# Both parts of the moving tokens in one 512-column pass, added up when the bank is read

## The chip, the cores and the metric

The kernel runs on one core of a Trainium2 chip. The metric is the device time of one launch in microseconds (us). TensorE (PE in the profile) does the matrix products out of on-chip memory into PSUM banks of 128 partitions by 512 float32 columns; VectorE (DVE), ScalarE (ACT) and GpSimd (POOL) work beside it, and DMA queues bring the weights from DRAM.

## What is computed

A trunk of four layers over 256 tokens of width 1024. Each layer has a mixer, a feed-forward part and a gated embedding, each with norms around it; the mixers are differential attention (layers 0 and 3), a sparse attention with compressed, selected and windowed keys (layer 1, "nsa") and an attention with forget gates (layer 2, "fox"). The change touches products of two kinds only, of all tokens with a weight matrix:

```python
# differential attention: q and k of 1024 columns each, v
q, k, v = jnp.split(h @ w_in, 3, axis=-1)
# nsa: queries, six key and value projections, gates
proj = h @ w_in
q = proj[..., :nq]
# blocks of 32 tokens are compressed by a small network
return jax.nn.gelu(blk @ w1) @ w2
# feed-forward: width 4096, squared relu
return jnp.square(jax.nn.relu(h @ w1)) @ w2
```

## The kernel before, in words

**Split products.** All values are float32. A factor is split into a high part (rounded to the engine's float32r form) and a low part (the rest), and `three` makes a product of a chunk of 128 rows out of three matmuls: high by high, low by high, high by low. Weights are split on the chip: a DMA brings a piece of 512 KB into a `raw` buffer, ACT copies the high part into `wh` (L148), DVE subtracts it for the low part `wl` (L149). Each engine takes its instructions in the order in which the program lists them.

**Tokens as the moving operand.** The transposed tokens lie in two tiles `hT` (high and low; tag `big`, 1024 features in KD = 8 chunks by 256 tokens). `lin_b` computes 256 columns of the result, transposed: two blocks of 128 columns, for each of them 8 chunks, for each chunk `three` with 128x128 weights standing and 256 token columns moving. The two blocks fill the two halves of one bank of tag `pj`. One ACT instruction reads the whole bank: L975 in the feed-forward part, L436 (`evac`) for q and k, L892 in nsa. `q_pair` of nsa does the same with its own weights. There are 78 such banks in a launch: 48 in the feed-forward part, 24 for q and k of the two differential layers and fox, 6 in nsa.

**Weights as the moving operand.** The out projection (`lin_a`), the second feed-forward matrix (`down`) and the gate have tokens standing and weight columns moving, 512 at a time. `up_tok` does the first feed-forward matrix in this way for the first two of eight groups of 512 columns, in two passes of 256 columns.

**Banks.** PSUM has 8 banks: 4 for `acc`, 2 for `pj`, 2 for `wk` (transposes and small products). In nsa `pj` also holds the sums of the compression (`compress_up`, L698) and of the attention's outputs.

**Order.** The order of an engine's instructions is fixed when the program is built. Strings such as `SEQ` give the order of projections and attention steps of a mixer; `LAG` says by how many products a transpose is put off so that its operands are ready. In the feed-forward part a group runs two `lin_b`, then 48 matmuls of `down` for the group before.

Of the kernel before, what the change touches and what calls it, by code (L numbers as in the profile page):

```python
# [12 lines left out]
F32R = mybir.dt.float32r  # L13
# [29 lines left out]
LAG = {0: {'o': ((0, 0), (27, 27)), 'd': ((6, 6), (10, 10)), 'g': ((0, 0), (0, 1)), 'u': ((15,), (10,)), 'i': ((0,), (2,))}, 1: {'o': ((10, 10), (24, 24)), 'd': ((9, 9), (10, 10)), 'g': ((0, 0), (0, 0)), 'u': ((13,), (12,)), 'i': ((13,), (1,))}, 2: {'o': ((10, 11), (24, 24)), 'd': ((10, 10), (7, 7)), 'g': ((0, 0), (9, 9)), 'u': ((15,), (13,)), 'i': ((0,), (1,))}, 3: {'o': ((0, 0), (27, 27)), 'd': ((6, 6), (14, 14)), 'g': ((0, 0), (0, 0)), 'u': ((15,), (10,)), 'i': ((0,), (0,))}}  # L43
# [43 lines left out]
class Trunk:  # L87
# [29 lines left out]
    def big(self, dt=F32R):  # L117
        return self.t([P, KD, S], "big", 4, dt)
# [38 lines left out]
    def unit(self, src, k0, nk, c0, nc):  # L157
        """Rows of chunks k0..k0+nk and columns c0..c0+nc, split: [128, nk, nc]."""
        v = src[k0 * P : (k0 + nk) * P, c0 : c0 + nc].rearrange("(c p) n -> p c n", p=P)
        return self.split(self.raw(v, [nk, nc]), [nk, nc])  # L160

    def panel(self, src, c0, nc, nk, early=()):
        """All of 1024 rows in units of nk chunks; [k] gives chunk k's parts [128, nc]."""
        us = list(early)
        us += [self.unit(src, k, min(nk, KD - k), c0, nc) for k in range(len(us) * nk, KD, nk)]
        return [tuple(z[:, k % nk, :] for z in us[k // nk]) for k in range(KD)]

    def three(self, out, l, r, first, last):
# [3 lines left out]
        mm(out, l[0], r[1], start=False, stop=last)  # L172
        for e in self.queue:
            e[0] -= 1
# [4 lines left out]
    def later(self, n, key, fn):  # L179
        """Runs fn, which fills a part of key's tiles, after n more products, to issue behind them."""  # L180
# [6 lines left out]
    def flush(self, keys):  # L187
        """Before keys' tiles are read: runs what still has to fill them."""
        while any(e[1] in keys for e in self.queue):
            self.queue.pop(0)[2]()  # L190

    def tok(self, aT, k, t):
        if self.queue:
            self.flush([(id(aT[0]), t)])
        return tuple(z[:, k, t * P : (t + 1) * P] for z in aT)
# [26 lines left out]
    def transpose_split(self, src, hi, lo, t, scale=None, n=KD, c0=0, lag=()):  # L222
        """src [128 tok, n*128] -> hi/lo[:, c0 + c, t*128:(t+1)*128]."""
# [23 lines left out]
    def rms_halves(self, halves):  # L247
        """1 / rms of [half 0, half 1]; each half's square is taken when it is ready."""
# [14 lines left out]
    def prenorm(self, t, g, hT, lag=()):  # L263
        """After the last change of x[t]; takes its halves one after the other."""
# [30 lines left out]
    def startnorm_(self, t, g, hT):  # L295
        """prenorm of the input as it arrives; the second step transposes."""
# [24 lines left out]
    def lin_a(self, src, c0, aT, done, mix, pj=False, cuts=None, early=()):  # L321
        """y[t] = a @ src[:, c0 : c0 + 1024]; token tile 0 runs before tile 1."""
# [12 lines left out]
    def mul_a(self, y, a, w, first, mix):  # L335
        """y += a @ w over a list of chunks. The last ones end the sum, its first half mix chunks ahead of its second."""
# [19 lines left out]

# [12 lines left out]
    def bias_rows(self):  # L369
        """The bias of every distance, one row per head, then once per query row at a pitch of SKEW."""  # L370
# [24 lines left out]
    def bias_blocks(self):  # L395
        """The bias of the compressed blocks: [query, head, block], kept in DRAM."""
# [12 lines left out]
    def bias_load(self, h0):  # L409
        """-bias and mask of heads h0..h0+3: [query, head, j], j the distance 128 + i - j."""  # L410
# [43 lines left out]
    def diff(self, i, ia, hT):  # L454
# [25 lines left out]
        oT = (self.big(), self.big())  # L480
# [51 lines left out]
    def scores(self, q, k, qs, w):  # L532
        """Negated scores of 4 heads; heads on different rows of the array go to different banks."""
# [7 lines left out]
    def pipeline(self, items):  # L541
        """Software pipeline over generators: each step starts one and moves every open one by a stage."""
# [7 lines left out]
    def heads(self, w_in, w_out, hT, item, seq):  # L550
        """Runs the steps of seq: q/k + pair projects, p does half of the embedding's product, b the block bias,
        Q/K + pair loads the weights of its projection, O a chunk of the output projection's, two digits start
        the item of a pair and a token tile."""
# [3 lines left out]
        def items():  # L557
            for z in seq.replace(".", " ").split():
                if z[0] in "qkQK":
# [7 lines left out]
                    self.evac(qk[u][:, w], self.lin_b(w_in, w * D + 256 * u, hT, ws[w, u]), 1.0 if w else -0.125)  # L567
# [13 lines left out]
    def fox(self, i, hT):  # L581
# [41 lines left out]
        oT = (self.big(), self.big())  # L623
# [43 lines left out]
    def split_out(self, o, oT, c0, n, t):  # L667
        oh, ol = [z[:, c0 : c0 + n, t * P : (t + 1) * P] for z in oT]
# [3 lines left out]
    def compress_blocks(self, kind, kT):  # L672
        """Blocks of 32 tokens, two tokens' 64 features on the partitions: [(token, d), pair, group, block of 16]."""
# [19 lines left out]
    def compress_up(self, kind, blk, ph):  # L693
        """First layer of the compression: [(group, block), hidden] on a half of the partitions."""
# [8 lines left out]
    def compress_gelu(self, ph):  # L703
        """gelu of both kinds' hidden layers, transposed: [hidden, half, kind, group, block of 32]."""
# [40 lines left out]
    def nsa(self, i, hT):  # L745
# [79 lines left out]
        oT = (self.big(), self.big())  # L825
# [12 lines left out]
        def q_pair(ap):  # L838
# [3 lines left out]
            for r2 in range(2):  # L842
                o = self.pj()
                for rr in range(2):
                    r = 2 * r2 + rr
                    for k in range(KD):
                        st = [z[:, r, 2 * (k % 2) : 2 * (k % 2) + 2, :].rearrange("p g d -> p (g d)") for z in us[k // 2]]
                        self.three(o[:, rr * S : (rr + 1) * S], st, self.both(hT, k), k == 0, k == KD - 1)
                nc.scalar.activation(q[:, 2 * r2 : 2 * r2 + 2, :].rearrange("p a b -> p (a b)"), o, AF.Copy, scale=-0.125)
# [40 lines left out]
        for z, c in ((0, 512), (1, 1024)):  # L890
            o = self.lin_b(w_in, C0 + c, hT)
            nc.scalar.activation(ksw[:, :, z, :], o.rearrange("p (a b) -> p a b", a=2), AF.Copy)  # L892
# [71 lines left out]
    def mlp(self, i, hT, done):  # L964
# [191 lines left out]
```

## Time and profile before

| | before |
|---|---|
| time, median of 3 runs | 1440.13 us (1440.06 to 1442.18) |
| profiled execution: span | 1449.6 us, 9.5 us over the median of the runs |
| TensorE matmuls | 1411.0 us, 97%, 8814 instructions |
| TensorE weight loads | 1225.6 us, 85% |
| VectorE | 855.8 us, 59%, 1495 instructions |
| ScalarE | 755.1 us, 52%, 1239 instructions |
| GpSimd | 71.9 us, 5% |

How to read it: the span is that of one execution under the profiler; no other time of that execution is recorded, so differences worked out from its rows are taken off or put onto the median of the runs. TensorE is busy nearly all of the time. A matmul's record runs from its start to the end of its passage through the array, and the next one starts before that, so records overlap; how long one holds the engine is read from the distance between starts.

### The profile page before, as it was taken

The page shows a single profiled execution, that of the slowest core. Times are in us where ns is not written, and L with a number is a line of the kernel's source. Part 1 is how long each engine was busy: PE and PEld are TensorE (multiplying, and loading weights), DVE is VectorE, ACT ScalarE, POOL GpSimd, SP SyncE. Part 2 cuts the span into 40 slices and gives each one's busy share as a digit, 9 for nine tenths or more (in the row PEclk, how much of TensorE's full clock was granted, in tenths as well). Part 3 has the DMA queues.
Part 4 walks back from the last instruction along what each step waited for, and adds up shares of the span by engine and source line. Part 5 has one row for each costly group of instructions (what it writes and reads, how often), then busy time and mean ns, then how long its engine had stood idle before and what let it go on. Part 6 is the DMA issues. An engine that isn't in the chain of part 4 may idle for free.

```text
span 1449.6 us, 22594 instructions
## 1 busy us (share of the span) xinstructions
PE 1411.0 (97%) x8814; PEld 1225.6 (85%) x8814; DVE 855.8 (59%) x1495; ACT 755.1 (52%) x1239; POOL 71.9 (5%) x116
## 2 busy tenths in 40 slices
PE   8589999999999999999999999999999999999998
PEld 6588898998888678998987987998988987999987
DVE  5265765556637656655566555755557577855545
ACT  4255555444625565554446555645446656644443
POOL 1000200000100001000001000000001001100000
PEclk9888999999999899999999999999999999999999
DMA  8564465655575204655645742765646643655642
GB/s 298 177 209 136 136 217 173 202 190 180 164 216 177 77 30 146 225 185 173 202 160 157 257 138 87 233 191 173 203 138 213 221 141 109 213 194 175 203 146 73
DMA packets 155042, 251.41 MB, mean 173 GB/s; under 512 B 10294, under 2 KB 119782, under 8 KB 154936
## 3 DMA queue, kind: packets, MB, share of 16 engines
q1 hardware_dynamic: 144312, 236.44, 50.1%
q10 hardware_dynamic: 10624, 13.53, 3.0%
q8 instruction: 69, 1.13, 0.3%
q14 instruction: 37, 0.30, 0.1%
HBM read 247.61 MB, written 4.43 MB: 174 GB/s over the span
## 4 chain that ended last, share of the span: by engine, by line
PE 68%; issue 21%; DMA 3%; POOL 3%; DVE 2%; ACTq 2%; ACT 2%; DVEq 0%; SPq 0%; POOLq 0%
PE pj L170 11%; PE pj L171 10%; PE pj L172 10%; PE acc L170 9%; PE acc L171 9%; PE acc L172 9%; PE wk L234 2%; PE acc L538 2%; DMA nb<-skew 2%; ACTq L383 2%; PE acc L907 1%; POOL small L213 1%; PE pj L698 1%; PE wk L513 1%; PE wk L658 1%
## 5 line engine op out<-in xcount | busy, mean ns | idle before, releaser
L149 DVE TENSOR_TENSOR wl<-raw,wh 128x1024 fp32r<-128x1024 f32 x421 | 509.9, 1221 | 356.4 <-ACT wh L148 342.6
L148 ACT ACTIVATE wh<-raw 128x1024 fp32r<-128x1024 f32 x421 | 441.9, 1057 | 364.4 <-PE acc L171 149.8
L170 PE MATMUL pj<-big,wh 128*128 128x256 f32 x1248 | 357.2, 286 | 11.8 <-ACT wh L148 11.8
L171 PE MATMUL pj<-big,wl 128*128 128x256 f32 x1248 | 356.2, 285 | 1.1 <-DVE wl L149 1.1
L172 PE MATMUL pj<-big,wh 128*128 128x256 f32 x1248 | 355.5, 285 | 0.0
L170 PEld LDWEIGHTS pj<-big,wh 128*128 128x128 f32 x1248 | 241.1, 193 | 16.2 <-ACT wh L148 12.3
L171 PEld LDWEIGHTS pj<-big,wl 128*128 128x128 f32 x1248 | 241.1, 193 | 5.0 <-DVE wl L149 2.2
L172 PEld LDWEIGHTS pj<-big,wh 128*128 128x128 f32 x1248 | 241.1, 193 | 0.3
L170 PE MATMUL acc<-wh,s 128*128 128x512 f32 x512 | 200.3, 391 | 0.0
L171 PE MATMUL acc<-wh,s 128*128 128x512 f32 x512 | 199.6, 390 | 0.0
L172 PE MATMUL acc<-wl,s 128*128 128x512 f32 x512 | 199.3, 389 | 0.0
L170 PE MATMUL acc<-wh,big 128*128 128x512 f32 (+2 forms) x344 | 132.0, 384 | 0.0
L171 PE MATMUL acc<-wh,big 128*128 128x512 f32 (+2 forms) x344 | 131.1, 381 | 0.0
L172 PE MATMUL acc<-wl,big 128*128 128x512 f32 (+2 forms) x344 | 130.3, 380 | 0.0
L172 PEld LDWEIGHTS acc<-wl,s 128*128 128x128 f32 x512 | 96.1, 188 | 20.3
L170 PEld LDWEIGHTS acc<-wh,s 128*128 128x128 f32 x512 | 96.2, 188 | 18.9
L171 PEld LDWEIGHTS acc<-wh,s 128*128 128x128 f32 x512 | 96.3, 188 | 18.8
L170 PE MATMUL pj<-wh,big 128*128 128x256 f32 (+1 forms) x320 | 100.3, 315 | 0.3 <-ACT big L241 0.2
L171 PE MATMUL pj<-wh,big 128*128 128x256 f32 (+1 forms) x320 | 98.7, 309 | 0.3 <-DVE big L242 0.3
L172 PE MATMUL pj<-wl,big 128*128 128x256 f32 (+1 forms) x320 | 98.3, 307 | 0.0
L432 ACT ACTIVATE s<-s,small 128x128 f32<-128x128 f32 (+1 forms) x160 | 70.7, 446 | 33.8 <-DVE small L428 29.2
L170 PEld LDWEIGHTS acc<-wh,big 128*128 128x128 f32 x344 | 65.6, 191 | 12.6 <-issue 1.0
(209 smaller groups left out, 1545.6 us busy)
## 6 DMA issues: line engine op xcount, KB each, us to landing
raw<-in_mlp_w_dram SPq DMA_DIRECT2D x256, 512.0 KB, 3.9
raw<-in_da_w_in_dram SPq DMA_DIRECT2D x48, 512.0 KB, 5.5
raw<-in_ple_gate_w_dram SPq DMA_DIRECT2D x32, 512.0 KB, 3.5
raw<-in_fox_w_in_dram SPq DMA_DIRECT2D x24, 512.0 KB, 4.1
raw<-in_nsa_w_in_dram SPq DMA_DIRECT2D x18, 512.0 KB, 4.7
g<-in_norm_g_dram SPq DMA_DIRECT2D x16, 512.0 KB, 5.3
raw<-in_da_w_out_dram SPq DMA_DIRECT2D x16, 512.0 KB, 3.3
nb<-skew ACTq DMA_DIRECT2D x12, 512.0 KB, 4.8
```

The lines of the kernel that those rows point to most:

```text
L148: self.nc.scalar.activation(wh, w, AF.Copy),
L149: self.nc.vector.tensor_tensor(wl, w, wh.bitcast(F32), op=ALU.subtract),
L170: mm(out, l[0], r[0], start=first, stop=False)
L171: mm(out, l[1], r[0], start=False, stop=False)
L172: mm(out, l[0], r[1], start=False, stop=last)
L213: nc.gpsimd.tensor_scalar(me, ms, EPS, 1.0, op0=ALU.add, op1=ALU.mult)
L234: z = nc.tensor.transpose(pt[:, c * P : (c + 1) * P], src[:, (b + c) * P : (b + c + 1) * P], self.ident)
L383: self.dq[QS[1]].dma_start(sk, src)
L432: nc.scalar.activation(e[:, b, :], e[:, b, :], AF.Exp, bias=m[:, b : b + 1], scale=-1.0, accum_out=s[:, b : b + 1])
L513: nc.tensor.matmul(po[:, hh * P : (hh + 1) * P], at[:, hh, kb, :], vs[kb][:, h * P : (h + 1) * P], start=kb == 0, stop=kb == nk - 1,)
L538: self.nc.tensor.matmul(sc[c][:, hh * w : (hh + 1) * w], q[cs, hh, qs], k[cs, hh, :w], start=True, stop=True)
L658: nc.tensor.matmul(po[c * HD : (c + 1) * HD, hh * P : (hh + 1) * P], vs[kb][:, h * HD : (h + 1) * HD], at[:, hh, kb, :], start=kb == 0, st ...
```

## The change

`pair` takes the place of `three` where tokens move. The high and the low part of the tokens become one tile of two planes, and the high weights meet both in one matmul of 2 x 256 columns, whose result fills the two halves of a bank; the low weights meet the high part in a second matmul of 256 columns, added to the first half. Each block of 128 result columns now has a `pj` bank of its own. ACT copies the second half out, then DVE adds the first half; in the feed-forward part the relu moves into the DVE instruction that squares. `up_tok` takes 512 weight columns in a pass. The numbers in `LAG` that count products of this kind are halved.

```diff
-    def big(self, dt=F32R):
-        return self.t([P, KD, S], "big", 4, dt)
+    def big(self):
+        z = self.t([P, 2, KD, S], "big", 2, F32R)
+        return z[:, 0], z[:, 1], z
...
+    def pair(self, out, l, aT, k, first, last):
+        mm = self.nc.tensor.matmul
+        a = self.both(aT, k)[0]
+        mm(out.rearrange("p (z n) -> p z n", z=2), l[0], aT[2][:, :, k, :], start=first, stop=False)
+        mm(out[:, :S], l[1], a, start=False, stop=last)
+        self.tick()
...
     def lin_b(self, src, c0, hT, w=None):
         if w is None:
             w = self.panel(src, c0, 256, 4)
-        o = self.pj()
         for b in range(2):
             bs = slice(b * P, (b + 1) * P)
+            o = self.pj()
             for k in range(KD):
-                self.three(
-                    o[:, b * S : (b + 1) * S], (w[k][0][:, bs], w[k][1][:, bs]), self.both(hT, k), k == 0, k == KD - 1,
-                )
-        return o
+                self.pair(o, (w[k][0][:, bs], w[k][1][:, bs]), hT, k, k == 0, k == KD - 1)
+            yield o
...
     def evac(self, dst, o, scale=1.0):
-        self.nc.scalar.activation(dst.rearrange("p a b -> p (a b)"), o, AF.Copy, scale=scale)
+        self.nc.scalar.activation(dst, o[:, S:], AF.Copy, scale=scale)
+        self.nc.vector.scalar_tensor_tensor(dst, o[:, :S], scale, dst, op0=ALU.mult, op1=ALU.add)
...
             for b in range(2):
-                o = self.lin_b(w1, 512 * gi + 256 * b, hT)
                 z = self.m2([P, 512])
-                nc.scalar.activation(z, o, AF.Relu)
+                for c, o in enumerate(self.lin_b(w1, 512 * gi + 256 * b, hT)):
+                    zc = z[:, c * S : (c + 1) * S]
+                    nc.scalar.activation(zc, o[:, S:], AF.Copy)
+                    nc.vector.tensor_tensor(zc, zc, o[:, :S], op=ALU.add)
                 q = self.m2([P, 512])
-                nc.vector.tensor_tensor(q, z, z, op=ALU.mult)
+                nc.vector.scalar_tensor_tensor(q, z, 0.0, z, op0=ALU.max, op1=ALU.mult)
...
-                w[gi] = [self.panel(w1, 512 * gi + 256 * b, 256, 4) for b in range(2)]
+                w[gi] = self.panel(w1, 512 * gi, 512, 2)
...
-                    for b in range(2):
-                        for k in range(KD):
-                            self.three(o[:, b * 256 : (b + 1) * 256], self.tok(hT, k, t), w[gi][b][k], k == 0, k == KD - 1)
+                    for k in range(KD):
+                        self.three(o, self.tok(hT, k, t), w[gi][k], k == 0, k == KD - 1)
```

In the changed program the weights' split is at L150 and L151 (148 and 149 before), `evac` at L448 (ACT) and L449 (DVE), the first step of the softmax at L439 (428 before), L704 is L690 of before, L646 and L647 are L632 and L633.

VectorE at the start of layer 0's attention, before: the low parts of the weights (`wl`), then the first step of the softmax, which reads the scores `acc` and the bias `nb`.

```order
L149 TENSOR_TENSOR wl_92_477<-raw_90_474,wh_91_476 128x1024
L149 TENSOR_TENSOR wl_95_483<-raw_93_480,wh_94_482 128x1024
L149 TENSOR_TENSOR wl_109_611<-raw_107_608,wh_108_610 128x1024
L428 ISA s4_99_494,small_100_495<-acc_97_488,nb_96_486 128x128
L428 ISA small_100_495 128x1
```

The same place now; pj_86 and pj_87 are the two blocks of k, pj_88 and pj_89 those of q.

```order
L449 SCALAR_TENSOR_TENSOR s4_85_371<-pj_86_372,s4_85_371 128x256
L449 SCALAR_TENSOR_TENSOR s4_85_371<-pj_87_391,s4_85_371 128x256
L151 TENSOR_TENSOR wl_92_451<-raw_90_448,wh_91_450 128x1024
L151 TENSOR_TENSOR wl_95_457<-raw_93_454,wh_94_456 128x1024
L151 TENSOR_TENSOR wl_111_561<-raw_109_558,wh_110_560 128x1024
L151 TENSOR_TENSOR wl_114_567<-raw_112_564,wh_113_566 128x1024
L449 SCALAR_TENSOR_TENSOR s4_85_371<-pj_88_410,s4_85_371 128x256
L151 TENSOR_TENSOR wl_135_618<-raw_133_615,wh_134_617 128x1024
L151 TENSOR_TENSOR wl_138_624<-raw_136_621,wh_137_623 128x1024
L449 SCALAR_TENSOR_TENSOR s4_85_371<-pj_89_429,s4_85_371 128x256
L439 ISA s4_99_468,small_100_469<-acc_97_462,nb_96_460 128x128
```

The addition of pj_88 stands behind four splits of weights, that of pj_89 behind two more, and the softmax behind all of them; ahead of the softmax there were three splits.

VectorE in nsa, before the compression, before: L690 adds the position embedding to keys and values that a DMA has laid out anew.

```order
L149 TENSOR_TENSOR wl_774_3981<-raw_772_3978,wh_773_3980 128x1024
L690 TENSOR_TENSOR s4_743_3802<-s4_742_3797,small_741_3795 128x16x15 x4
L690 TENSOR_TENSOR s4_748_3819<-s4_747_3814,small_746_3812 128x16x15
L149 TENSOR_TENSOR wl_777_3987<-raw_775_3984,wh_776_3986 128x1024
L690 TENSOR_TENSOR s4_748_3819<-s4_747_3814,small_746_3812 128x16x15 x3
```

The same place now; pj_773, pj_774, pj_781 and pj_782 are the four blocks of the two projections (`ksw`) that TensorE runs there, in this order, out of the two `pj` banks.

```order
L151 TENSOR_TENSOR wl_790_3615<-raw_788_3612,wh_789_3614 128x1024
L704 TENSOR_TENSOR s4_758_3461<-s4_757_3456,small_756_3454 128x16x15 x4
L449 SCALAR_TENSOR_TENSOR s4_766_3486<-pj_773_3499,s4_766_3486 128x256
L449 SCALAR_TENSOR_TENSOR s4_766_3486<-pj_774_3518,s4_766_3486 128x256
L704 TENSOR_TENSOR s4_763_3478<-s4_762_3473,small_761_3471 128x16x15
L151 TENSOR_TENSOR wl_793_3621<-raw_791_3618,wh_792_3620 128x1024
```

The additions of pj_773 and pj_774 stand behind the four L704 that wait for DMAs.

VectorE at the start of fox's attention now; pj_1491, 1492, 1500, 1501 and 1514 are blocks in TensorE's order, and L646 waits for the DMA of `nb`.

```order
L449 SCALAR_TENSOR_TENSOR s4_1490_6924<-pj_1491_6925,s4_1490_6924 128x256
L151 TENSOR_TENSOR wl_1530_7142<-raw_1528_7139,wh_1529_7141 128x1024
L449 SCALAR_TENSOR_TENSOR s4_1490_6924<-pj_1492_6944,s4_1490_6924 128x256
L646 TENSOR_TENSOR m2_1520_7117<-nb_1519_7115,mid_1441_6702 128x512
L647 TENSOR_TENSOR nb_1519_7115<-nb_1519_7115,mid_1441_6702 128x4x128
L151 TENSOR_TENSOR wl_1533_7148<-raw_1531_7145,wh_1532_7147 128x1024
L449 SCALAR_TENSOR_TENSOR s4_1499_6975<-pj_1500_6976,s4_1499_6975 128x256
```

Before, a split of weights stood ahead of the two bias instructions and another behind them, with no addition between; now the addition of pj_1500 stands behind the two and a split.

## Rows read from the trace of the kernel before

**Rows 1.** Page of the profile, parts 1 and 4: busy time, chain.
```profile
PE 1411.0 (97%) x8814; PEld 1225.6 (85%) x8814; DVE 855.8 (59%) x1495; ACT 755.1 (52%) x1239; POOL 71.9 (5%) x116
PE 68%; issue 21%; DMA 3%; POOL 3%; DVE 2%; ACTq 2%; ACT 2%; DVEq 0%; SPq 0%; POOLq 0%
```
**Rows 2.** Groups by line and shape: matmuls of lin_b, down and up_tok.
```profile
L170 PE MATMUL pj<-big,wh 128*128 128x256 f32 x1248 | 357.2, 286 | 11.8 <-ACT wh L148 11.8
L170 PE MATMUL acc<-wh,s 128*128 128x512 f32 x512 | 200.3, 391 | 0.0
L170 PE MATMUL pj<-wh,big 128*128 128x256 f32 x256 | 73.6, 288 | 0.2 <-ACT big L241 0.2
```
**Rows 3.** ACT timeline, feed-forward: start, us, instruction, [idle before <-releaser].
```profile
303.01 0.60 ACT L975 ACTIVATE m<-pj 128x512 f32<-128x512 f32 x1 [0.33 <-PE pj L172]
...
307.38 1.06 ACT L148 ACTIVATE wh<-raw 128x1024 fp32r<-128x1024 f32 x1 [2.17 <-PE pj L172]
308.77 0.60 ACT L975 ACTIVATE m<-pj 128x512 f32<-128x512 f32 x1 [0.33 <-PE pj L172]
...
325.43 0.60 ACT L975 ACTIVATE m<-pj 128x512 f32<-128x512 f32 x1 [0.33 <-PE pj L172]
```
**Rows 4.** Groups by line and shape: ACT and DVE on 256 columns.
```profile
L508 ACT ACTIVATE m<-wk 128x256 f32<-128x256 f32 x8 | 3.1, 383 | 3.5 <-PE wk L506 3.5
L501 DVE SCALAR_TENSOR_TENSOR s<-s,small 128x256 f32<-128x256 f32 x16 | 7.0, 479 | 0.1
L518 DVE TENSOR_TENSOR mid<-wk,small 128x256 f32<-128x256 f32 x16 | 6.8, 423 | 19.1 <-PE wk L513 19.1
```
**Rows 5.** Stretches of 3 us: busy time by engine, granted clock, DMA.
```profile
48.00:51.00 3.00, 0.00 (x0) 0.00 (x0) 0.00 (x0) 0.00 (x0) 0.00 (x0) 0.50 0.26 100
60.00:63.00 3.00, 3.00 (x23) 3.00 (x22) 1.35 (x2) 0.00 (x0) 0.00 (x0) 0.79 1.05 363
90.00:93.00 3.00, 3.00 (x20) 3.00 (x19) 1.69 (x8) 1.09 (x6) 0.00 (x0) 0.67 0.93 322
```
**Rows 6.** Timeline of PE in layer 0: products of q, scores, transposes.
```profile
55.61 0.58 PE L170 MATMUL pj<-big,wh 128*128 128x256 f32 x1 [11.84 <-ACT wh L148]
...
69.28 0.71 PE L538 MATMUL acc<-s 64*128 64x128 f32 x8 [1.73 <-ACT s L436]
...
83.28 0.74 PE L506 MATMUL wk<-ident,s 128*128 128x128 f32 x2 [3.75 <-DVE s L501]
```
**Rows 7.** Timelines of DVE and ACT in layer 0.
```profile
55.59 5.77 DVE L149 TENSOR_TENSOR wl<-raw,wh 128x1024 fp32r<-128x1024 f32 x5 [23.55 <-ACT wh L148]
...
71.10 1.06 ACT L148 ACTIVATE wh<-raw 128x1024 fp32r<-128x1024 f32 x1 [1.88 <-DMA raw<-in_da_w_in_dram]
74.37 1.06 ACT L148 ACTIVATE wh<-raw 128x1024 fp32r<-128x1024 f32 x1 [2.21 <-DMA raw<-in_da_w_in_dram]
...
78.23 1.04 ACT L148 ACTIVATE wh<-raw 128x1024 fp32r<-128x1024 f32 x1
```
**Rows 8.** Timelines of DVE and PE in nsa.
```profile
414.19 2.18 DVE L690 TENSOR_TENSOR s<-s,small 128x240 f32<-128x240 f32 x4 [6.13 <-DMA s<-s]
...
416.63 7.09 PE L698 MATMUL pj<-raw,s 128*64 128x256 f32 x32 [0.43 <-DVE s L690]
```
**Rows 9.** Timelines of ACT and DVE at the start of fox's attention.
```profile
812.21 0.60 ACT L436 ACTIVATE s<-pj 128x512 f32<-128x512 f32 x1 [0.33 <-PE pj L172]
...
808.21 1.23 DVE L149 TENSOR_TENSOR wl<-raw,wh 128x1024 fp32r<-128x1024 f32 x1 [5.11 <-ACT wh L148]
811.90 0.69 DVE L632 TENSOR_TENSOR m<-nb,mid 128x512 f32<-128x512 f32 x1 [2.46 <-DMA nb<-crow]
813.11 1.22 DVE L149 TENSOR_TENSOR wl<-raw,wh 128x1024 fp32r<-128x1024 f32 x1
```
**Rows 10.** Timelines of ACT and DVE at the start of layer 3's attention.
```profile
1150.96 0.60 ACT L436 ACTIVATE s<-pj 128x512 f32<-128x512 f32 x1 [0.38 <-PE pj L172]
...
1145.23 1.23 DVE L149 TENSOR_TENSOR wl<-raw,wh 128x1024 fp32r<-128x1024 f32 x1 [0.89 <-ACT wh L148]
```

More of the change, by code (lines that the diff above doesn't have):

```diff
@@ L42 @@
 MIXS = {0: {'v': 3, 'o': 2, 'd': 0, 'g': 0}, 1: {'v': 6, 'o': 2, 'd': 8, 'g': 1}, 2: {'v': 3, 'o': 6, 'd': 1, 'g': 0}, 3: {'v': 6, 'o': 2, 'd': 0, 'g': 0}}
-LAG = {0: {'o': ((0, 0), (27, 27)), 'd': ((6, 6), (10, 10)), 'g': ((0, 0), (0, 1)), 'u': ((15,), (10,)), 'i': ((0,), (2,))}, 1: {'o': ((10, 10), (24, 24)), 'd': ((9, 9), (10, 10)), 'g': ((0, 0), (0, 0)), 'u': ((13,), (12,)), 'i': ((13,), (1,))}, 2: {'o': ((10, 11), (24, 24)), 'd': ((10, 10), (7, 7)), 'g': ((0, 0), (9, 9)), 'u': ((15,), (13,)), 'i': ((0,), (1,))}, 3: {'o': ((0, 0), (27, 27)), 'd': ((6, 6), (14, 14)), 'g': ((0, 0), (0, 0)), 'u': ((15,), (10,)), 'i': ((0,), (0,))}}
+LAG = {0: {'o': ((0, 0), (13, 13)), 'd': ((6, 6), (10, 10)), 'g': ((0, 0), (0, 1)), 'u': ((7,), (5,)), 'i': ((0,), (2,))}, 1: {'o': ((10, 10), (12, 12)), 'd': ((9, 9), (10, 10)), 'g': ((0, 0), (0, 0)), 'u': ((6,), (6,)), 'i': ((13,), (1,))}, 2: {'o': ((10, 11), (12, 12)), 'd': ((10, 10), (7, 7)), 'g': ((0, 0), (9, 9)), 'u': ((7,), (6,)), 'i': ((0,), (1,))}, 3: {'o': ((0, 0), (13, 13)), 'd': ((6, 6), (14, 14)), 'g': ((0, 0), (0, 0)), 'u': ((7,), (5,)), 'i': ((0,), (0,))}}
 ST_N = 4
@@ L172, in three, with tick @@
         mm(out, l[0], r[1], start=False, stop=last)
+        self.tick()
[4 more added lines that the diff above has]
+        mm(out[:, :S], l[1], a, start=False, stop=last)
+        self.tick()
+    def tick(self):
         for e in self.queue:
@@ L194, in tok @@
             self.flush([(id(aT[0]), t)])
-        return tuple(z[:, k, t * P : (t + 1) * P] for z in aT)
+        return tuple(z[:, k, t * P : (t + 1) * P] for z in aT[:2])
     def both(self, aT, k):
@@ L479, in diff @@
         nc.vector.scalar_tensor_tensor(nlam, le[:, 1:2], -lam_init, le[:, 0:1], op0=ALU.add, op1=ALU.subtract)
-        oT = (self.big(), self.big())
+        oT = self.big()
         def item(u, t, q, k, shared):
@@ L566, in items @@
                         qk[u] = self.s4([P, 2, 2, S])
-                    self.evac(qk[u][:, w], self.lin_b(w_in, w * D + 256 * u, hT, ws[w, u]), 1.0 if w else -0.125)
+                    for b, o in enumerate(self.lin_b(w_in, w * D + 256 * u, hT, ws[w, u])):
+                        self.evac(qk[u][:, w, b], o, 1.0 if w else -0.125)
                 elif z == "O":
@@ L622, in fox @@
         self.dq[QS[4]].dma_start(crow, cs)
-        oT = (self.big(), self.big())
+        oT = self.big()
         def item(u, t, q, k, shared):
@@ L667, in split_out @@
     def split_out(self, o, oT, c0, n, t):
-        oh, ol = [z[:, c0 : c0 + n, t * P : (t + 1) * P] for z in oT]
+        oh, ol = [z[:, c0 : c0 + n, t * P : (t + 1) * P] for z in oT[:2]]
         self.nc.scalar.activation(oh, o, AF.Copy)
@@ L824, in nsa @@
         blks = [self.compress_blocks(kind, kvT[:, 2 * kind : 2 * kind + 2, :]) for kind in range(2)]
-        oT = (self.big(), self.big())
+        oT = self.big()
         q_ws = {}
@@ L842, in q_pair @@
             for r2 in range(2):
-                o = self.pj()
                 for rr in range(2):
                     r = 2 * r2 + rr
+                    o = self.pj()
                     for k in range(KD):
                         st = [z[:, r, 2 * (k % 2) : 2 * (k % 2) + 2, :].rearrange("p g d -> p (g d)") for z in us[k // 2]]
-                        self.three(o[:, rr * S : (rr + 1) * S], st, self.both(hT, k), k == 0, k == KD - 1)
-                nc.scalar.activation(q[:, 2 * r2 : 2 * r2 + 2, :].rearrange("p a b -> p (a b)"), o, AF.Copy, scale=-0.125)
+                        self.pair(o, st, hT, k, k == 0, k == KD - 1)
+                    self.evac(q[:, r, :], o, -0.125)
                 yield
@@ L890, in nsa @@
         for z, c in ((0, 512), (1, 1024)):
-            o = self.lin_b(w_in, C0 + c, hT)
-            nc.scalar.activation(ksw[:, :, z, :], o.rearrange("p (a b) -> p a b", a=2), AF.Copy)
+            for b, o in enumerate(self.lin_b(w_in, C0 + c, hT)):
+                self.evac(ksw[:, b, z, :], o)
             fill(z - 3)
@@ L1069, in run @@
         self.early = []
-        hT = (self.big(), self.big())
+        hT = self.big()
         for t in range(2):
@@ L1101, in run @@
             g1, g2 = self.g_row(i, 1), self.g_row(i, 2)
-            hT = (self.big(), self.big())
+            hT = self.big()
             def mixed(t, y):
@@ L1110, in run @@
             g3 = self.g_row(i, 3)
-            xT = (self.big(), self.big())
+            xT = self.big()
             def fed(t, y):
@@ L1119, in run @@
             if not last:
-                hT = (self.big(), self.big())
+                hT = self.big()
                 g0 = self.g_row(layers[li + 1], 0)
```

## Prediction

> **What bounds the kernel now.** I read the page first: TensorE is busy for 1411.0 us of a span of 1449.6, VectorE for 59% of it, ScalarE for 52%, and the chain that ended last is 68% TensorE, with 21% of issue, in which an engine waited for nothing that the profile shows [rows 1]. So a matmul that goes away comes back as time unless something else ends last in its place. How much it is worth can't be read from a matmul's record: 286 ns for 256 columns and 391 ns for 512 [rows 2] overlap. It is read from ScalarE's timeline in the feed-forward part, where each bank is read 0.33 us after TensorE finishes it. Two reads of two `lin_b` in a row start at 303.01 and 308.77, so 48 matmuls of 256 columns take 5.76 us, 0.120 each. The next read is 16.66 later, at 325.43; less one `lin_b` that leaves 10.90 us for the 48 matmuls of `down`, 0.227 each [rows 3]. Twice the columns cost 1.89 times as much: each matmul has a fixed part of about 13 ns (2 x 0.120 - 0.227).
>
> **What the change takes away.** A product goes from 3 x 0.120 = 0.360 to 0.227 + 0.120 = 0.347 us. There are 1248 such products [rows 2], one matmul less in each. `up_tok` has 256 products of 256 columns [rows 2], which become 128 of 512: 384 matmuls less. Together 1632 x 12.9 ns = **-21.0 us**, which agrees with the count of instructions that the change leaves (8814 - 1632). The price of the 512 pass is that of `down`, whose moving columns are one run of 512; here they are two runs of 256 in two planes, which no row shows. The bounds are 0.227 and two passes of 256 (0.240); at the upper one the 16 us of `lin_b` are gone. I take 0.227, because 256 and 512 columns differ by 0.107 us, just what 256 columns need at 2.4 GHz, so the columns set the pace and not the start of a run.
>
> A rule speaks against the size of this. The Trainium skill, "TensorE: Matmul & The Clock Gate", section "Back-to-back issue gap", gives a stream's distance as columns / 2.4 plus about 2.5 ns, so a matmul spared would bring 2.5 ns and not 13, and the whole change 4.1 us. The rows differ from it: 0.120 and 0.227 are each some 13 ns over the columns' time [rows 3], and I keep the rows' price in the sum.
>
> **What it adds.** Per `lin_b`, ScalarE has two copies of 256 columns (2 x 0.383) in place of one read of 512 (0.60), and VectorE two additions (0.42 each in the feed-forward part, 0.48 with the scale) [rows 3, 4]. Over 78 banks that is 13 us for ScalarE and some 69 us for VectorE, which goes to 64% busy. On average both have room. What costs time is where the additions stand: VectorE takes its instructions in order, there are two `pj` banks, and a bank that waits for an addition queued behind something late stops TensorE. Before, VectorE had no part in freeing these banks. I looked at each place where in the new order an addition stands behind an instruction that waits in the trace.
>
> *Layer 0.* ScalarE comes out of its DMA issues late, and the first q product starts at 55.61 after an idle of 11.84 us [rows 6]. Now q's first block also needs the bank of k's first block, whose addition follows four of the five splits that begin at 55.59 (4 x 1.15, so 60.2) [rows 7]: it starts at about 60.65, 5 us later. The clock is at 0.50 in that idle, and with a mean of 0.79 in 60 to 63 it came back at 61.3, after some 4.4 us of matmuls at half speed; that costs 2.2 us and is paid again. Both q blocks end near 68.5. The first scores need the addition of pj_88, behind a split whose weights arrive at 71.10: 71.10 + 1.06 + 1.23 + 0.48 = 73.9; then that of pj_89, behind splits of the weights of 74.37 and of about 78 [rows 7]: 80.5. In between only 13 matmuls of the next block fit. After 80.5 the other 51 of those four blocks are left, 8.8 us at full speed and 1 to 2 more for the clock, so the transposes that started at 83.28 [rows 6] start near 91. The 7.7 us are not all lost: before, TensorE ran at half speed from 83.28 to about 92 (clock 0.67 in 90 to 93 [rows 5]) after a wait of 3.75, and lost 2 to 2.5 us, which a TensorE that had no wait there keeps. **+5.5**, between +3 and +8.
>
> *Layer 1, the key projections of nsa.* VectorE reaches the four L704 and waits for DMAs until 414.19; they last 2.18 [rows 8], and the additions of pj_773 and pj_774 stand behind them: 416.85 for the first. TensorE has finished these two blocks by then, as the second projection started before at about 416.63 - 0.43 - 5.76 = 410.4 [rows 3, 8], and the third block needs a bank. It runs its 5.55 us from 416.85 on and the compression starts at 422.4 in place of 416.63: +5.8. An idle of over 6 us is longer than the 3.75 us after which the clock was down in layer 0, so 2.2 us of half speed come on top. **+8.0**; 5.6 if the clock holds, 10 if the two blocks begin later still.
>
> *Layer 1, queries.* The compression's sums hold one `pj` bank and the attention's outputs later on, so query blocks there follow each other in one bank. Each then shows copy and addition, 0.38 + 0.48 = 0.86 us [rows 4] and two handovers. One such place is bare and two are partly covered: **+2.0**, between 0.9 and 3.
>
> *Fox.* The first block starts at 812.21 - 0.33 - 11.52 = 800.4, the second ends at 806.0. The addition of pj_1492 stands behind a split that ends at 809.44, so pj_1501, ready at 808.75, starts at 809.85: +1.1. The addition of pj_1500 stands behind the bias instructions, which wait for a DMA until 811.90, and behind a split from 813.11 to 814.34 [rows 9]: 814.75 against 812.6, +2.1. **+3.2**, between 1 and 4.
>
> *Layer 3.* The second `lin_b` ended at 1150.96 - 0.38 = 1150.6, and the first began 11.5 us before, at 1139.1; its two blocks now end at 1144.65. The first addition stands behind the split of 1145.23 to 1146.46 [rows 10] and ends at 1146.9. **+2.2**, between 1 and 3.
>
> *Feed-forward.* In each of 24 groups the fourth block needs the bank of the second, whose addition stands behind a split of weights that the second block itself releases: 1.06 + 1.23 + 0.42 = 2.7 us after its end [rows 3, 4, 7], when the third block takes 2.78. I take **0**; a handover of 0.2 more in each would be +5.
>
> The sum is -21.0 + 5.5 + 8.0 + 2.0 + 3.2 + 2.2 = **-0.1 us**. It is made against the profiled execution, whose span lies 9.5 us over the median of the runs; I put it onto the median, 1440.13, as nothing in these places belongs to the profiling. A change within 0.2% (2.9 us) can't be told from none here.
>
> **The rivals.**
> (a) *The stalls are mostly not there.* VectorE is busy 59% of the time, and weights may arrive earlier when TensorE waits, which brings the splits and the additions forward. For it speaks that three of the five places hang on DMA times of one execution; against it, that in nsa and fox the DMAs are issued by ScalarE before the point that moves. With 4 to 10 us of stalls left: 1423 to 1429; with none 1419.1.
> (b) *The forecast*: the five places give back what the matmuls bring, 1436 to 1444.
> (c) *Slower: the feed-forward banks.* If the handovers of the chain release, wh, wl, addition exceed the margin of 0.08 us between 2.70 and 2.78, every group stalls in the same way, 24 x 0.2 = 5 us, and 0.4 would be 10: 1445 to 1450. It decides from about 0.15 us per group on. For it speaks how small the margin is; against it, that the bank is asked for only once the weights of the fourth block are there too.
> (d) *The wide pass is not cheaper.* Two runs at 0.240 leave only up_tok's 5 us against the same stalls: 1456. Against it stands the price of 512 columns in `down`. The skill's 2.5 ns per matmul (the section above) would give 1440.1 - 4.1 + 20.9 = 1457; the trace does not bear it out.
>
> **How the numbers follow.** (a) 0.27, (b) 0.45, (c) 0.20, (d) 0.08, of which 0.03 for the skill's rule. The likeliest is (b), with its sum: **1440.0 us**, its own range 1436 to 1444. The low ends of the five places (3 + 5.6 + 0.9 + 1 + 1) would give 1430.6, the high ones with the feed-forward's 5 give 1452; the range of 1429 to 1452 leaves out (d) and the lower part of (a). Faster by over 0.2% (below 1437.3): (a) and 0.06 of (b), 0.33. Slower (over 1443.0): (c), (d) and 0.08 of (b), 0.36. Within: 0.31.
>
> **What would show it.** In the feed-forward part, reads of banks 5.55 us apart for two blocks together and no wait of a matmul for an addition: the first term and (c). In layer 0, scores that wait for an addition until about 74 and 80, and transposes near 91. In nsa, a wait of over 5 us of the third key block for VectorE, and a clock of 0.50 behind it. In fox, two waits of 1 and 2 us. I am wrong if the waits for additions (L449 and the feed-forward's) add up to under 10 us or over 28, if the clock does not fall in nsa, or if a 512-column pass on the tokens takes other than 0.227.

## The result and the profile after

The changed kernel takes 1463.99 us (median of 4 runs, 1458.17 to 1465.51) against 1441.16 for the kernel before; the ratio is 1.0132, 95% interval 1.0106 to 1.0158. Run once more beside three experiments it gave 1.0106 (1.0087 to 1.0126). So the change costs 1.1 to 1.3%, some 15 to 19 us; 1440.0 was wrong, and so was its range to 1452. One execution of the kernel before, of 1710.83 us at a mean clock of 0.747, was in the slow state and is in none of the ratios.

The page of the changed kernel, part 1, beside [rows 1]:

```profile
PE 1398.2 (96%) x7182; PEld 1133.3 (78%) x7182; DVE 921.1 (63%) x1651; ACT 768.3 (53%) x1317; POOL 70.4 (5%) x116
```

The 1632 matmuls are gone, and VectorE and ScalarE have 65 and 13 us more. The forecast had 69 and 13; the additions with the scale took 0.42 us each and not 0.48. The span is 1456.4 us, only 6.8 over that of before. That pair of executions misleads: the profiled one of before was slower than any of its timed ones (1449.6 us of span, where they have a median near 1441), and the profiled one of after was its kernel's fastest. Times below are therefore compared over all runs.

TensorE's own timeline of the changed kernel shows where it waits for the new additions (L449); each row is the matmul that ends the wait, with the wait in brackets, beside [rows 6, 8]:

```profile
57.79 0.80 PE L181 MATMUL pj<-big,wh 128*128 128x512 f32 x1 [15.19 <-DVE s L449]
70.97 0.80 PE L551 MATMUL acc<-s 64*128 64x128 f32 x4 [5.24 <-DVE s L449]
77.18 0.49 PE L551 MATMUL acc<-s 64*128 64x128 f32 x4 [0.95 <-DVE s L449]
...
127.07 0.72 PE L181 MATMUL pj<-big,wh 128*128 128x512 f32 x1 [3.25 <-DVE s L449]
...
417.21 0.80 PE L181 MATMUL pj<-big,wh 128*128 128x512 f32 x1 [5.74 <-DVE s L449]
...
813.22 0.50 PE L181 MATMUL pj<-big,wh 128*128 128x512 f32 x1 [1.44 <-DVE s L449]
817.03 0.50 PE L181 MATMUL pj<-big,wh 128*128 128x512 f32 x1 [0.73 <-DVE s L449]
...
1152.34 0.50 PE L181 MATMUL pj<-big,wh 128*128 128x512 f32 x1 [1.23 <-DVE s L449]
...
1207.74 0.50 PE L181 MATMUL pj<-big,wh 128*128 128x512 f32 x1 [3.22 <-DVE s L449]
```

The places that the prediction named are there: layer 0 (three rows), nsa (417.21, forecast 416.85), fox (two), layer 3 (1152.34). Two were not named, 127.07 and its twin in layer 3, 1207.74. What stands ahead of the addition there is seen on VectorE and, in the last line, on ScalarE, whose copy has to come first:

```profile
122.03 0.42 DVE L531 TENSOR_TENSOR mid<-wk,small 128x256 f32<-128x256 f32 x1 [1.80 <-PE wk L526]
122.38 1.22 DVE L151 TENSOR_TENSOR wl<-raw,wh 128x1024 fp32r<-128x1024 f32 x1
...
124.08 1.23 DVE L151 TENSOR_TENSOR wl<-raw,wh 128x1024 fp32r<-128x1024 f32 x1
125.22 0.42 DVE L439 CUSTOM_DVE_ANT_0 s<-acc,nb 128x256 f32<-128x256 f32 x1
...
126.59 0.75 DVE L449 SCALAR_TENSOR_TENSOR s<-pj,s 128x256 f32<-128x256 f32 x2
...
125.36 0.66 ACT L448 ACTIVATE s<-pj 128x256 f32<-128x256 f32 x2
```

VectorE waits there once, 1.80 us for TensorE, and has a queue of work for the rest (splits, four softmax steps). ScalarE comes late too. TensorE had issued the last product of both blocks by 118.1, and ScalarE copies them out at 125.36, behind splits and reads of `acc`. Had the first addition followed its copy at once, it would have started at 125.74 (a copy takes 0.38 us) and not at 126.59; so VectorE's queue makes some 0.85 us of the 3.25, by this estimate, and ScalarE's the rest.

The same block in the kernel before did not wait:

```profile
118.55 0.28 PE L170 MATMUL pj<-big,wh 128*128 128x256 f32 x1
...
121.37 0.59 ACT L436 ACTIVATE s<-pj 128x512 f32<-128x512 f32 x1
```

It started at 118.55, while the bank of the two blocks ahead of it was read only at 121.37. Two blocks shared a bank, so the two `pj` banks held four; now each block has its own, and they hold two.

What a wait costs afterwards is in the windows of the changed kernel (busy time by engine, granted clock, DMA). A granted clock of 0.50 is 1.2 GHz, 1 is 2.4 GHz:

```profile
126.00:129.00 3.00, 1.93 (x6) 1.64 (x7) 2.96 (x11) 1.98 (x9) 0.18 (x2) 0.70 0.85 251
129.00:132.00 3.00, 3.00 (x15) 2.64 (x14) 1.08 (x3) 0.29 (x1) 0.00 (x0) 0.74 0.93 323
...
417.00:420.00 3.00, 2.79 (x9) 2.40 (x10) 3.00 (x7) 0.00 (x0) 0.00 (x0) 0.50 0.01 3
420.00:423.00 3.00, 3.00 (x17) 2.61 (x17) 1.63 (x5) 0.68 (x2) 0.00 (x0) 0.88 0.60 175
...
1209.00:1212.00 3.00, 3.00 (x12) 2.58 (x11) 1.72 (x5) 0.00 (x0) 0.00 (x0) 0.53 0.53 166
```

After each of the waits over 3 us TensorE runs at 1.2 GHz for some 3 to 5 us, in or shortly after them (a window with a mean between 0.50 and 1 has a part at either level), the two unnamed ones included.

In the feed-forward part ScalarE's reads of the banks show the pace, as in [rows 3]. One group is four blocks and one `down`:

```profile
233.89 0.39 ACT L990 ACTIVATE m<-pj 128x256 f32<-128x256 f32 x1 [1.93 <-PE pj L182]
237.62 0.36 ACT L990 ACTIVATE m<-pj 128x256 f32<-128x256 f32 x1
239.61 0.38 ACT L990 ACTIVATE m<-pj 128x256 f32<-128x256 f32 x1 [1.62 <-PE pj L182]
243.39 0.36 ACT L990 ACTIVATE m<-pj 128x256 f32<-128x256 f32 x1
256.24 0.39 ACT L990 ACTIVATE m<-pj 128x256 f32<-128x256 f32 x1 [1.93 <-PE pj L182]
```

From the first read to the first of the next group it is 22.35 us; 20 such groups take 22.23 to 22.35, 22.30 on average. Before it was 5.76 + 16.66 = 22.42 [rows 3]; by the price of the prediction it would be 10.90 + 32 x 0.347 = 22.0. The reason is seen on TensorE, at the starts of the wide matmuls:

```profile
235.46 0.40 PE L181 MATMUL pj<-big,wh 128*128 128x512 f32 x1
235.69 0.28 PE L182 MATMUL pj<-big,wl 128*128 128x256 f32 x1
235.81 0.40 PE L181 MATMUL pj<-big,wh 128*128 128x512 f32 x1
...
236.17 0.40 PE L181 MATMUL pj<-big,wh 128*128 128x512 f32 x1
...
236.52 0.40 PE L181 MATMUL pj<-big,wh 128*128 128x512 f32 x1
...
236.87 0.40 PE L181 MATMUL pj<-big,wh 128*128 128x512 f32 x1
```

From 235.46 to 236.87 four products take 1.41 us, 0.353 each, and not 0.347.

### The profile page after: what moved, and what is told of

Same layout as the page of the kernel before. It is cut to its first block, busy times and chain, and to the rows that moved or that the text cites. A ratio compares the mean times of both kernels' runs of the same rounds, so it can differ in the third digit from the quotient of the medians.

```text
span 1456.4 us, 19597 instructions
## 1 busy us (share of the span) xinstructions
PE 1398.2 (96%) x7182; PEld 1133.3 (78%) x7182; DVE 921.1 (63%) x1651; ACT 768.3 (53%) x1317; POOL 70.4 (5%) x116
## 5 line engine op out<-in xcount | busy, mean ns | idle before, releaser
L151 DVE TENSOR_TENSOR wl<-raw,wh 128x1024 fp32r<-128x1024 f32 x421 | 510.2, 1221 | 243.9 <-ACT wh L150 232.8
L150 ACT ACTIVATE wh<-raw 128x1024 fp32r<-128x1024 f32 x421 | 442.5, 1058 | 220.5 <-PE acc L173 104.0
L181 PE MATMUL pj<-big,wh 128*128 128x512 f32 x1248 | 458.9, 409 | 30.8 <-DVE s L449 30.8
L181 PEld LDWEIGHTS pj<-big,wh 128*128 128x128 f32 x1248 | 239.2, 192 | 98.1 <-DVE s L449 33.5
L990 ACT ACTIVATE m<-pj 128x256 f32<-128x256 f32 x96 | 36.0, 374 | 85.6 <-PE pj L182 85.6
L172 PE MATMUL pj<-wh,big 128*128 128x512 f32 x192 | 78.1, 409 | 0.0
L174 PE MATMUL pj<-wl,big 128*128 128x512 f32 x192 | 76.0, 396 | 0.6 <-DVE wl L151 0.6
L173 PE MATMUL pj<-wh,big 128*128 128x512 f32 x192 | 75.7, 394 | 0.0
L172 PEld LDWEIGHTS acc<-wh,big 128*128 128x128 f32 x344 | 65.0, 189 | 12.3 <-issue 1.0
L173 PEld LDWEIGHTS acc<-wh,big 128*128 128x128 f32 x344 | 65.1, 189 | 11.1
```

The lines of the kernel that those rows point to most:

```text
L150: self.nc.scalar.activation(wh, w, AF.Copy),
L151: self.nc.vector.tensor_tensor(wl, w, wh.bitcast(F32), op=ALU.subtract),
L172: mm(out, l[0], r[0], start=first, stop=False)
L173: mm(out, l[1], r[0], start=False, stop=False)
L181: mm(out.rearrange("p (z n) -> p z n", z=2), l[0], aT[2][:, :, k, :], start=first, stop=False)
L990: nc.scalar.activation(zc, o[:, S:], AF.Copy)
```

## The experiments

Every time is compared with runs of the kernel before on the same chip. "Less the clock" is the mean over the runs of time multiplied by granted clock, a rough estimate of what the time would be if TensorE never left 2.4 GHz (rough, since the granted clock is an average over idle time too); it is 1421 for the kernel before in each of the four groups of runs.

| kernel | ratio to before (95%) | clock | less the clock, us |
|---|---|---|---|
| before | 1 | 0.983 to 0.985 | 1420.7 to 1421.5 |
| changed, again (x13) | 1.0106 (1.0087 to 1.0126) | 0.978 | 1428.5 |
| x1 tokens in one run | 1.0107 (1.0075 to 1.0139) | 0.977 | 1426.7 |
| x2 feed-forward only | 0.9955 (0.9933 to 0.9977) | 0.984 | 1415.1 |
| x3 attention only | 1.0140 (1.0113 to 1.0167) | 0.979 | 1433.9 |
| x4 up_tok only | 0.9975 (0.9955 to 0.9995) | 0.984 | 1417.5 |
| x5 wide, then narrow | 1.0066 (1.0046 to 1.0086) | 0.975 | 1419.6 |
| x6 reads first | 1.0072 (1.0045 to 1.0098) | 0.979 | 1426.9 |
| x9 nsa's order | 1.0082 (1.0056 to 1.0108) | 0.978 | 1425.7 |
| x8 x5, x6, x9 together | 1.0041 (1.0017 to 1.0064) | 0.979 | 1420.8 |
| x10 ScalarE frees the bank | 1.0048 (1.0033 to 1.0063) | 0.979 | 1419.8 |
| x11 x10 and x5 | 0.9975 (0.9962 to 0.9988) | 0.981 | 1414.4 |
| x12 x2 and x5 | 0.9917 (0.9893 to 0.9940) | 0.983 | 1408.9 |
| x14 x2, two by two | 0.9924 (0.9901 to 0.9947) | 0.981 | 1408.2 |

**Which part loses: x2, x3, x4.** x2 keeps `three`, one bank for two blocks and one ScalarE read in the attention, x3 keeps them in the feed-forward part, x4 is the kernel before with this alone, and the numbers in `LAG` halved as in the change:

```diff
-                w[gi] = [self.panel(w1, 512 * gi + 256 * b, 256, 4) for b in range(2)]
+                w[gi] = self.panel(w1, 512 * gi, 512, 2)
...
-                    for b in range(2):
...
+                        self.three(o, self.tok(hT, k, t), w[gi][k], k == 0, k == KD - 1)
```

> The paired product in the feed-forward part alone (with up_tok's 512 columns); attention has the old products, banks and reads. Theory (stalls in the attention make the loss): no wait for an addition over 1 us is left, and the feed-forward part gives up_tok's 5 us and 2 to 3 us of the groups that the trace shows (22.31 to 22.36 us against 22.42): 1433 to 1435. By the forecast's price of 0.347 it would be 1426. Rival (the feed-forward banks or a lower clock there make the loss): 1445 or more.

> The paired product in the attention alone; the feed-forward part is that of before. Theory (stalls in layer 0 and nsa, and the half clock that follows them): the loss is here, 15 to 30 us, 1456 to 1471, with the waits of about 15, 5 and 6 us for L449 as in the changed kernel. Rival (feed-forward makes the loss): within 5 us of before.

> The kernel before with up_tok's 512 columns alone (and the halved numbers in LAG). By 384 matmuls less at 12.9 ns the time falls by 5 us, to 1436. Rival (weight loads or the splits of the weights set the pace there): no change.

The whole loss is in the attention (x3, +1.4%). The feed-forward part gains 0.45%, a little less than was expected of x2, and up_tok alone gives 0.25%. Less the clock, up_tok gives 4.0 us, near the 5.0 of the forecast; the paired product of the feed-forward part adds 2.4 to it, where the forecast had 48 x 0.206 = 9.9. The intervals of x2 and x4 overlap, so the 2.4 rests on the groups of the trace: 22.28 us on average in x2 against 22.42, 3.4 us in 24 groups.

**What makes a pair dear: x1, x5, x14.** x1 lays the planes side by side, x5 changes the order of a block's matmuls:

```diff
-        z = self.t([P, 2, KD, S], "big", 2, F32R)
+        z = self.t([P, KD, 2, S], "big", 2, F32R)
```

```diff
+    def block(self, out, ls, aT):
+        for k, l in enumerate(ls):
+            mm(out.rearrange("p (z n) -> p z n", z=2), l[0], aT[2][:, :, k, :], start=k == 0, stop=False)
+        for k, l in enumerate(ls):
+            mm(out[:, :S], l[1], aT[0][:, k, :], start=False, stop=k == KD - 1)
```

> The changed kernel, with the two planes of the tokens laid side by side for each chunk, so that the 512 moving columns are one run. In the changed kernel's trace a product of lin_b holds TensorE 0.347 us in some blocks and 0.353 in most. Theory (two runs): the second run costs the step of 0.0067 us; then all blocks take 0.347 here, and the time falls by 6 to 8 us against the changed kernel (to about 1456). Rival (weights or banks decide it): the pitch stays at 0.353 in the same blocks and the time stays at 1464.

> The changed kernel, with the order of a block's matmuls changed: first the eight of 512 columns, then the eight of 256, in place of wide and narrow in turn. In the changed kernel's trace the distance from wide to wide runs in a cycle of 0.349, 0.350, 0.361 us in most blocks. Theory (the turn from wide to narrow costs it): a block takes 8 x 0.227 + 8 x 0.120 = 2.78 us here, 0.05 less than 2.83, which over 156 blocks is 6 to 8 us off the changed kernel. Rival (weights, banks or other engines set the pace): a block stays at 2.83 and the time within 3 us of the changed kernel.

x1's time shows no change (1.0107 beside 1.0106 for the changed kernel, which ran on another chip). Its interval reaches 4.6 us either way, where a fall of 6 to 8 was expected, so the pace of its groups decides:

```profile
235.58 0.39 ACT L990 ACTIVATE m<-pj 128x256 f32<-128x256 f32 x1 [1.93 <-PE pj L182]
...
257.87 0.39 ACT L990 ACTIVATE m<-pj 128x256 f32<-128x256 f32 x1 [1.93 <-PE pj L182]
```

They take 22.29 us here, and 22.29 on average (22.30 in the changed kernel): two runs are not the reason. x5 takes 0.4 points off the ratio, on another chip than x13. Combined with the feed-forward version it is the cleanest:

> The paired product in the feed-forward part alone, wide ones ahead of narrow ones, up_tok's 512 columns; attention as before. Theory (the turn from wide to narrow): groups of 22.06 us in place of 22.34, 24 times, so 6.7 us less than the feed-forward version with wide and narrow in turn (0.9955): 0.990 to 0.992 of before. Rival: 0.9955 as that one.

ScalarE's reads of one group in x12:

```profile
229.23 0.38 ACT L1014 ACTIVATE m<-pj 128x256 f32<-128x256 f32 x1 [1.88 <-PE pj L193]
232.12 0.37 ACT L1014 ACTIVATE m<-pj 128x256 f32<-128x256 f32 x1
234.88 0.39 ACT L1014 ACTIVATE m<-pj 128x256 f32<-128x256 f32 x1 [2.39 <-PE pj L193]
237.71 0.37 ACT L1014 ACTIVATE m<-pj 128x256 f32<-128x256 f32 x1
251.29 0.38 ACT L1014 ACTIVATE m<-pj 128x256 f32<-128x256 f32 x1 [1.88 <-PE pj L193]
```

22.06 us from first to first: the price of the forecast (22.0), and 0.9917 of before (expected 0.990 to 0.992). This version beats both kernels. The groups average 22.05 us and those of x2 22.28: the same instructions in another order are worth 0.23 us in each of 24 groups, 5.5 us, and the ratio fell by as much (0.9955 to 0.9917).

x14 takes two wide ones, then two narrow ones, four times in a block:

> The feed-forward version with two wide matmuls, then two narrow ones, four times in a block. Theory (each turn between wide and narrow costs): half as many turns as one by one, so groups of four blocks and down lie halfway between 22.06 us (eight by eight) and 22.34 (one by one), near 22.2, and the time is 3 us over that of eight by eight. Rival (a cycle of three, as one by one has it, comes only from one by one, since a wide pass there meets a load in the wrong place): 22.06 as eight by eight.

Its groups take 22.09 us (for instance 229.97 to 252.06), far from halfway, and the time is that of x12 within the interval. So the loss does not grow in step with the number of turns between wide and narrow; strict alternation has something of its own. What that is these runs do not settle.

**Who holds the bank: x10, x11.** ScalarE copies both halves out, and VectorE adds from the copy:

```diff
-        self.nc.scalar.activation(dst, o[:, S:], AF.Copy, scale=scale)
-        self.nc.vector.scalar_tensor_tensor(dst, o[:, :S], scale, dst, op0=ALU.mult, op1=ALU.add)
+        e = self.m2([P, 512])
+        self.nc.scalar.activation(e, o, AF.Copy, scale=scale)
+        self.nc.vector.tensor_tensor(dst, e[:, :S], e[:, S:], op=ALU.add)
```

> The changed kernel, with a bank freed by ScalarE alone: it copies both halves (128x512) to a buffer, and VectorE adds them up from there. Matmuls, banks and the number of additions are those of the changed kernel. Theory (banks held until VectorE's addition make the loss): no product of lin_b waits for VectorE any more; waits for additions are left at the scores alone, up to 6 us in layer 0; 10 to 18 us less than the changed kernel, 1.000 to 1.006 of before. Rival (VectorE's additional 66 us or ScalarE's place make the loss): within 4 us of the changed kernel.

> The same, with the eight wide matmuls of a block ahead of the eight narrow ones. If the two parts of the loss are apart, 6 to 8 us less than with ScalarE freeing the bank alone: 0.995 to 1.001 of before.

The waits of x10 on TensorE (in total, times, longest):

```profile
PE pj L181 <- ACT m L449: 17.2, 3, 14.6
PE acc L552 <- DVE s L450: 5.3, 2, 3.2
```

L449 and L450 of x10 are the copy and the addition. No product of `lin_b` waits for VectorE now; 127 and 1207 are gone, layer 0 still begins late (14.6 us, before 11.84 [rows 6]) since ScalarE itself comes late there, and the scores still wait for additions. The ratio falls from 1.0106 to 1.0048 on the same chip, with as many additions and a larger copy for ScalarE. So a release by ScalarE alone is worth 0.58%, 8.4 us, with no work taken off either engine. It is not VectorE's queue alone that this takes away: the program's order came out anew with the edit, and ScalarE's copies at the place of 127 now start at 123.61, ahead of two splits, and not at 125.36. No run parts the two. With x5's order (x11) it is 0.9975: a version with the pair everywhere can beat the kernel before, but not the one that leaves the attention alone.

**Reordering instead: x6, x9, x8.** x6 raises the priority of copies and additions in the listing, x9 lists nsa's position additions behind the additions of its first two blocks, x8 joins x5, x6 and x9 and lets GpSimd issue nsa's DMAs.

```diff
+        with self.tc.high_priority():
             self.nc.scalar.activation(dst, o[:, S:], AF.Copy, scale=scale)
             self.nc.vector.scalar_tensor_tensor(dst, o[:, :S], scale, dst, op0=ALU.mult, op1=ALU.add)
```

> The changed kernel, with ScalarE's copies and VectorE's additions of the blocks put ahead of what is ready at the same time (splits of weights, softmax steps). Theory (the order on VectorE makes the stalls): the waits of 3.25 us near 127 and 3.22 near 1207 and those of 15.2, 5.2 and 1.0 in layer 0 shrink to under 1, 0 and 13, the half clock behind them goes, and the time falls by 10 to 16 us against the changed kernel; nsa's wait of 5.7 stays. Rival (the additions delay what now comes after them as much): within 4 us of the changed kernel.

> The changed kernel, with nsa's position additions listed behind the additions of the first key projection's two blocks. The copies on ScalarE still stand behind its DMA issues, which end at 413.8. Theory: the third block starts at about 414.8 in place of 417.2, so 2.5 us less, up to 4.5 with a shorter half clock. Rival (the compression sets the pace there): no change.

> The changed kernel with the three edits together (wide then narrow, reads first, nsa's order), and nsa's DMAs issued by GpSimd and not by ScalarE. If the parts add up, 20 to 28 us less than the changed kernel: 1 to 9 us faster than before. If the loss lies elsewhere, over 1450.

x6 helps at the start of layer 0, and misses at 127 and 1207, where the wait grows:

```profile
54.48 1.22 PE L181 MATMUL pj<-big,wh 128*128 128x512 f32 x2 [11.48 <-ACT wh L150]
...
124.86 0.79 PE L181 MATMUL pj<-big,wh 128*128 128x512 f32 x1 [4.26 <-DVE s L450]
```

On VectorE of x6 four splits in place of three now stand ahead of that addition. x9 does what was expected of it, the third block at 414.67 and the compression at 420.86 (417.21 and 424.56 in the changed kernel):

```profile
414.67 0.50 PE L181 MATMUL pj<-big,wh 128*128 128x512 f32 x1 [2.70 <-DVE s L449]
...
420.86 7.09 PE L715 MATMUL pj<-raw,s 128*64 128x256 f32 x32 [0.28 <-issue]
```

It could not do more, since in the changed kernel ScalarE has its own part in that wait. It copies the two blocks out at 413.82, behind the issue of eight DMAs:

```profile
408.37 5.40 ACTq L698 DMA_DIRECT2D s<-s  x8
413.82 0.66 ACT L448 ACTIVATE s<-pj 128x256 f32<-128x256 f32 x2 [5.48 <-DMA s<-s]
```

x9's time, 1.0082, can't be told from the changed kernel's 1.0106, nor can x6's, since the intervals meet. x8 is slower than its parts promised: nsa's wait is back at 5.62 us, as ScalarE's copy of the block now stands behind a split whose weights came at 412.32 and behind another copy until 413.55.

**The control.**

> The changed kernel itself, on the chip of the three others, so that they can be compared with it: 1.013 of before, as it was.

It gave 1.0106 (1.0087 to 1.0126), a little under the first measurement, with an interval that meets it; x10 to x12 are read against this one, since they ran on its chip.

## Why the prediction was wrong

It was made of a gain of 21.0 us and losses of 20.9. Of the losses 19.4 were waits and lateness and 1.5 clock (1.5 in layer 0 and 2.2 in nsa, less 2.2 taken back in layer 0). The runs part this in two ways.

By parts (means, chip of x2 and x3): the feed-forward part gave 6.2 us where the forecast had 5.0 + 9.9 = 14.9, and the attention cost 20.9 where it had 20.9 - 6.2 = 14.7. Over half of the error is in the part that has next to no waits.

By terms: taken over all runs on the chip of x13, the changed kernel is 16.1 us over the kernel before (means 1460.7 and 1444.6). The matmuls gave an estimated 9.6 us and not 21.0 (next point). TensorE idles 1456.4 - 1398.2 = 58.2 us in the profiled execution and idled 38.6 in that of before [rows 1], 19.6 more (58.1 in x13 and 37.4 in x2, whose attention is the old one). That leaves some 6 us for the clock, an estimate. So the sum of the waits was right, and that was luck in part: two places that I had not named made up for places that came out smaller.

By my own signs I was wrong too: the waits for L449 add up to 30.8 us for products and 6.2 for scores, over the 28 that I had set (11.84 of them stood there before as a wait for ScalarE).

- **The price of the pair, the step that failed first.** "A product goes from 0.360 to 0.227 + 0.120 = 0.347" added up two prices read from streams of one width. In alternation a product takes 0.353, and in most groups the fourth block waits a little for the bank of the second (10.90 + 32 x 0.3533 is 22.21; the groups average 22.30, the one shown has 0.14 more; with ScalarE freeing the bank, in x10, most take 22.23). Of the 21.0 us, up_tok gave 4.0 (forecast 5.0), the feed-forward pair 2.4 (9.9), and the attention's 480 products, at 0.0067 each less than before, an estimated 3.2 (6.2): 9.6 in all. That the 512-column pass itself is cheap was right: x12 has the forecast's groups. The upper bound that I named for the wide pass, 0.240, was close to what it takes on average in alternation (0.353 less some 0.117 for the narrow one), and I put aside rival (d) for it with a chance of 0.08; its reason, two runs, x1 shows wrong. Rival (d)'s 1456 and the 1457 beside it lie nearest to the time, in part by luck, since the two missed waits are in neither. The 1457 goes by the 2.5 ns of the Trainium skill, "TensorE: Matmul & The Clock Gate", section "Back-to-back issue gap", for each matmul spared. The runs do not agree with it: x12 spares 1152 matmuls, 2.9 us by that rule, and gained 11.3 (means).
- **Layer 0: right in kind, over in size.** 57.79, 70.97 and 77.18 in place of 60.65, 73.9 and 80.5; the transposes began at 86.71, 3.4 us later than before and not 7.7. (The 0.33 us read as TensorE's lead over a bank's read is ScalarE's idle in brackets; the prices are differences of reads and do not hang on it.)
- **nsa: right in time, half right in cause.** A wait of 5.74, half clock behind it, the compression at 424.56 in place of 416.63: +7.9, forecast +8.0. But only 2.5 us of it hang on the L704, as x9 shows; the rest is ScalarE's copy behind its DMA issues, which the forecast did not have. The query blocks, forecast +2.0, show no wait.
- **Fox and layer 3: right in place, a little smaller.** 2.2 against 3.2, and 1.2 against 2.2.
- **Missed: 127 and 1207.** I looked for additions behind an instruction that *waits* in the trace of before. Here copy and addition stand behind work that hardly waits, on both engines, and two banks that hold two blocks in place of four are too few for it: 6.5 us of waits, and half clock behind both. The estimate was made by a search for late events, and a busy queue is not one. In the profiled executions of x2 and of the changed kernel, whose feed-forward parts are alike, the first paired bank of layer 0's feed-forward part is read at 205.09 and 211.66, 6.6 us later, and layer 3 loses 5.6 between its neighbours; the forecast, matmuls spared counted, had 3.9 and 0.6.
- **The clock.** I counted it in layer 0 and nsa, and took back in layer 0 what the wait of before had cost. Over the runs the mean went from 0.9835 to 0.978, 8 us of time by that average, idle time counted in; that is 5 to 7 us more than I had, by the two estimates. That was no single fall: between 440 and 500 us, in nsa, TensorE is at 1.2 GHz for 0 to 20 us in the profiled executions of the five kernels with the old attention and for 10 to 20 in the ten with the new one.
- **Rival (c)** named a stall at each group's fourth block with 0.2 us; it is 0.09 on average, some 2 us.

## What to carry to other kernels

Read the price of a matmul from a stream that has the mix of widths you are going to issue; a price read between neighbours of the same width need not hold in alternation, and the order of independent matmuls can be worth as much as their number (x2 and x12: 5.5 us from the order alone). Count how many results the banks hold after a change, and not only how many banks there are. When a bank's release moves to an engine with a queue of other work, list everything that stands ahead of the release in that queue, busy or waiting, and hold it against the time until the bank is asked for again. If the release must pass two engines, try letting the less loaded one empty the bank alone and doing the sum from the copy; here that was worth 8.4 us.

## What the runs showed of the hardware

Wide and narrow passes one by one took 0.353 us a product in most blocks, and 0.347 in some (77.82 to 83.4 in layer 0 of the changed kernel), with the same operands' layout; eight by eight and two by two, a group of 32 products was 0.23 and 0.20 us shorter on average (22.28 us in x2, 22.05 in x12, 22.08 in x14). Laying the two planes out as one run of 512 columns made no difference. The kernel before itself varies from 1440 to 1453 us between executions, along with a mean clock from 0.988 to 0.978.
